# One-core encoder layer: projection weights planned in one list and loaded one projection ahead, and the last convolution chunk's taps in one piece

## The chip, the cores and the metric

The kernel runs on one core of one Trainium2 chip. The metric is the device time of one execution in microseconds (us). TensorE is called PE, VectorE DVE, ScalarE ACT, GpSimd POOL; SP issues the transfers (DMAs).

## What is computed

One encoder layer over 1552 tokens of 1024 channels: 16 meta tokens, a prompt of 512 and a sample of 1024, with shared weights. Cut to what matters:

```python
u = rms_norm(h, pre_g)
z = einsum('bld,de->ble', u, w_in)
c_val, c_glu, c_gate, q, k, v, a_gate = split(z)          # seven blocks of 1024 columns
conv_out = swish(layer_norm(dwconv31(c_val * sigmoid(c_glu)) + conv_b)) * silu(c_gate)
o_meta, o_grid = neighbourhood_attention(q, k, v, rel_bias)
att = concat(o_meta, o_grid) * silu(a_gate)
return h + rms_norm(concat(conv_out, att) @ w_out, post_g)
```

All is fp32. The products are made of split operands: an operand is rounded to a high part, and what is missing is its low part; each product is three matmuls (high·high, low·high, high·low).

## The kernel before

**Stages** (times of the span). Until 42 us the tokens are normalised and transposed; from 42 to 691 us the convolution branch runs; from 691 to 1222 us eight pairs of heads, each with its k and q projections, scores, softmax and weighted sum (`po`); from 1222 us the output product.

**A projection.** `w_in` is used in blocks of 128 output columns, each a weight of 512 KB. `load_w` (line 120) issues its transfer into `wraw` (SP), ACT casts it to the high part `whi` (line 115), POOL subtracts to get the low part `wlo` (line 116). `wraw`, `whi` and `wlo` have two buffers each, so a third weight waits until the first of the three has been used up. `proj` (line 128) then runs 24 matmuls into one PSUM tile `mm`, in the order high, low, high for each of 8 slices. Numbers below: val c is block c, glu c block 8+c, c_gate c block 16+c, q p block 24+p, k p block 32+p, a_gate p block 40+p ("ag p").

**The convolution stage.** Eight chunks of 128 channels. `conv_proj` (line 180) makes glu (4 tiles of 272, 256, 512 and 512 tokens, each through a sigmoid `sg` on ACT) and val (4 tiles, multiplied with `sg` into `ub` by DVE). `conv_taps` (line 218) is a 31-tap convolution: tap 0 by ACT (line 221), the other 30 by DVE, each reading the `z` the one before has written (line 223). `conv_stats` (line 237) subtracts a mean (`zc`, DVE), squares it (`zq`, ACT) and adds both into `acc` and `accsq`, on POOL or DVE. While DVE runs chunk c's taps, PE runs `stream(c)` (line 373): fillers (v units, c_gate, and ag 0 to 6) for about 44 us, then glu and val of chunk c+1. In chunk 7 the rest of the fillers run: two tiles of ag3, then ag4, ag5 and ag6.

**The last chunk** (line 388). For chunks 1 to 6 the taps are one piece, 128x1536. In chunk 7 `LASTP` makes two pieces: tokens 0 to 511 (128x512), whose statistics go to POOL, and 512 to 1535 (128x1024), whose statistics go to DVE.

**The end of the stage** (lines 419 to 426): six matmuls `ss` sum `acc` and `accsq` over channels; the rows leave through ACT and SP to `std`. The attention of a pair needs its k and q, the bias tables (`raw` from `ed`, added to `e` and `ei` by POOL, line 500) and v tiles (`vp`, `vt`, lines 528 and 531).

**What sets the order.** The Python code walks the work in the order above, with a generator for PE's side (`stream`) and one for DVE's (`convolve`), advanced by rough costs in us. A scheduler then places each engine's instructions by its own modelled times, so that the order on an engine can differ from that of the code; each engine runs its own list in order, and waits on semaphores.

Of the kernel before, what the change touches and what calls it, by code (L numbers as in the profile page):

```python
# [23 lines left out]
NPAIR = 8  # L24
# [4 lines left out]
MGROUPS = ((0, 272), (272, 528), (528, 1040), (1040, 1552))  # L29
# [11 lines left out]
NCG1 = 6  # L41
HOLD, EM1, NEW = 1, 13, 4
MLT = 1
NVS = 7
FILL = (0, 44, 44, 44, 44, 44, 44, 999)
NAG1 = 7
NXT = 4
LASTP = ((0, 1), (1, 3))
LAG = 1
IVM = 3  # L50
TAP_US = 1.85
CONV_ORDER = tuple((k, i) for k in "gv" for i in range(4))
BMM, BSS, BTP = 3, 2, 2
VPB = 1
# [13 lines left out]
def tile_encoder(ctx: ExitStack, tc: tile.TileContext, mt, xn, w_main, w_v, wo, cw, cb, lg, lb, pg, postg, rbt, rmask, y):  # L68
    nc = tc.nc
# [50 lines left out]
    def load_w(ec):  # L120
# [4 lines left out]
        split_w(raw, hi, lo)  # L125
        return hi, lo

    def proj(ps, hi, lo, c0, c1):
        n = c1 - c0
        uh, ul = u_cols(c0, c1)  # L130
        for dc in range(DC):
            for i, (w, u) in enumerate(((hi, uh), (lo, uh), (hi, ul))):
                nc.tensor.matmul(ps[:, :n], lhsT=w[:, dc, :], rhs=u[dc // 4][:, dc % 4, :],  # L133
                                 start=(dc == 0 and i == 0), stop=(dc == DC - 1 and i == 2))
# [40 lines left out]
    um = vpool.tile([128, DC, 32], F32, name="um")  # L175
    nc.gpsimd.memset(um, 0.0)
    ubs = [cpool.tile([128, 3, UBS], F32, name=f"ub{i}") for i in range(2)]
    w0 = {}

    def conv_proj(c, order):  # L180
        ub = ubs[c % 2]
        gh, gl = w0.pop(8 + c) if 8 + c in w0 else load_w(8 + c)
        val = [w0.pop(c) if c in w0 else None]
        sgs = {}

        def glu(i):
            c0, c1 = MGROUPS[i]
            psg = ps_mm.tile([128, 512], F32, name="mm", tag="mm")
            proj(psg, gh, gl, c0, c1)
            sgs[i] = cpool.tile([128, c1 - c0], F32, name=f"sg{i}")  # L190
            nc.scalar.activation(out=sgs[i], in_=psg[:, :c1 - c0], func=AF.Sigmoid)

        def value(i):
            if val[0] is None:
                val[0] = load_w(c)
            c0, c1 = MGROUPS[i]
            sg = sgs.pop(i)
            psv = ps_mm.tile([128, 512], F32, name="mm", tag="mm")
            proj(psv, *val[0], c0, c1)
            for name, a, b, off in pieces(c0, c1):  # L200
                if name == "m":
                    nc.vector.tensor_tensor(out=ub[:, 0, 0:15], in0=psv[:, 1:16], in1=sg[:, 1:16], op=ALU.mult)
                    nc.gpsimd.tensor_copy(out=ub[:, 1, 0:15], in_=ub[:, 0, 0:15])
                    continue
                seg = "pab".index(name)
                b0, nb = off // 64, (b - a) // 64
                o = ub[:, seg, 15:527].rearrange("p (r b c) -> p b r c", r=8, b=8)[:, b0:b0 + nb]
                nc.vector.tensor_tensor(out=o, in0=psv[:, a:b].rearrange("p (b r c) -> p b r c", r=8, c=8),
                                        in1=sg[:, a:b].rearrange("p (b r c) -> p b r c", r=8, c=8), op=ALU.mult)

        for kind, i in order:
            (glu if kind == "g" else value)(i)
            if kind == "v" and i == 3:
                nc.gpsimd.tensor_copy(out=ub[:, 1, 527:542], in_=ub[:, 2, 15:30])
                nc.gpsimd.tensor_copy(out=ub[:, 2, 0:15], in_=ub[:, 1, 512:527])
            yield 24 * (MGROUPS[i][1] - MGROUPS[i][0]) * 0.00045
# [10 lines left out]
    def new_z():  # L227
        return zpool.tile([128, 3, 512], F32, name="z", bufs=2)
# [64 lines left out]
                yield 2.8  # L293

    def c_gate(cs):
        ws = [load_w(16 + c) for c in cs]
        if cs[0] < 3:
            vws[cs[0] + 1] = load_v(cs[0] + 1)
            v_meta(cs[0] + 1, vws[cs[0] + 1][0])
        for g in range(3):  # L300
            for c, (wh, wl) in zip(cs, ws):
                ps = ps_mm.tile([128, 512], F32, name="mm", tag="mm")
                proj(ps, wh, wl, 16 + g * 512, 16 + g * 512 + 512)
                gt = gpool.tile([128, 512], F32, name="ag", tag="ag", bufs=2)
                nc.scalar.copy(out=gt, in_=ps)
                nc.sync.dma_start(cgd[g][c], gt)
                yield 5.5

    def a_gate(p):
        wah, wal = load_w(40 + p)  # L310
        for g in range(3):
            ps = ps_mm.tile([128, 512], F32, name="mm", tag="mm")
            proj(ps, wah, wal, 16 + g * 512, 16 + g * 512 + 512)
            gt = gpool.tile([128, 512], F32, name="ag", tag="ag", bufs=2)
            nc.scalar.copy(out=gt, in_=ps)
            nc.sync.dma_start(agd[g][p], gt)
            yield 5.5
# [12 lines left out]
    fill = fillers()  # L330
# [8 lines left out]
    with tc.tile_pool(name="start", bufs=2, side="right", reuse_waits="tile") as sp:  # L339
        gb = sp.tile([128, D], F32, name="gb", bufs=1)  # L340
        for i, s in enumerate((1, 0) + tuple(range(2, 13))):
            prenorm(s, sp, gb)
            if i == 0:
                vws[0] = load_v(0)
                vraw0 = vws[0][0]
            if i == IVM:
                v_meta(0, vraw0)
            if LAG <= i < LAG + NVS:
                next(fill)
            if s == 5:  # L350
                w0[8] = load_w(8)
                w0[0] = load_w(0)
        for dst, src in ((cw_sb, cw), (cb_sb, cb), (lg_sb, lg), (lb_sb, lb), (rm_sb, rmask)):
            nc.sync.dma_start(dst, src)
    zpool = es1.enter_context(tc.tile_pool(name="zpool", bufs=1, reuse_waits="tile"))
# [3 lines left out]
    z = new_z()  # L359
# [12 lines left out]

    def stream(c):

        t = 0.0
        while t < FILL[c]:
            dt = next(fill, None)
            if dt is None:
                break
            t += dt  # L380
            yield dt
        if c < 7:
            yield from conv_proj(c + 1, CONV_ORDER)

    def convolve(c, z):

        if c > 0:
            for a, b in ((0, 3),) if c < 7 else LASTP:
                for _ in conv_taps(c, z, a, b):
                    yield TAP_US * (b - a) / 3  # L390
                if c == 7:
                    for i in range(a, b):
                        conv_stats(c, z, i, nc.vector if b == 3 else nc.gpsimd)
        else:
            conv_mean(z)
        if c < 7:
            for i in range(3):
                conv_stats(c, z, i, nc.gpsimd)
                yield TAP_US / 3
        if 1 <= c <= 6:  # L400
            expand_bias(c - 1, last_load[0])

    for c in range(8):
        if c > 0:
            z = new_z()
# [56 lines left out]
    last = [None]  # L462

    def pair_proj(p):
        wkh, wkl = load_w(32 + p)
        pool = apool if p % 2 else kpool
        kh = pool.tile([128, 8, NROW, 8], F32R, name="kh")
        kl = pool.tile([128, 8, NROW, 8], F32R, name="kl")
        for (c0, c1) in MGROUPS:
            ps = ps_mm.tile([128, 512], F32, name="mm", tag="mm")  # L470
            proj(ps, wkh, wkl, c0, c1)
            for name, a, b, off in pieces(c0, c1):
                if name == "m":
                    src = ps[:, 0:16].rearrange("p (x c) -> p x c", x=2).unsqueeze(1).broadcast_to([128, 4, 2, 8])
                    for row in (ROW_M, ROW_M2):
                        oh = kh[:, :, row, :].rearrange("p (y x) c -> p y x c", x=2)
                        ol = kl[:, :, row, :].rearrange("p (y x) c -> p y x c", x=2)
                        nc.scalar.copy(out=oh, in_=src)
                        nc.vector.tensor_tensor(out=ol, in0=src, in1=oh.bitcast(F32), op=ALU.subtract)
                    continue  # L480
                row = {"p": ROW_P, "a": ROW_A, "b": ROW_B}[name]
                b0, nb = off // 64, (b - a) // 64
                src = ps[:, a:b].rearrange("p (b x) -> p b x", x=64)
                oh = kh[:, b0:b0 + nb, row:row + 8, :].rearrange("p b r c -> p b (r c)")
                ol = kl[:, b0:b0 + nb, row:row + 8, :].rearrange("p b r c -> p b (r c)")
# [91 lines left out]
    for p in range(NPAIR):  # L577
        e_build(p)
        kh, kl = pair_proj(p)
        wqh, wql = load_w(24 + p)  # L580
        for g in range(3):
            qs = pair_q(p, wqh, wql, g)
            attention(p, g, kh, kl, qs)
        if p >= NAG1:
            for _ in a_gate(p):
                pass
# [195 lines left out]
```

## Time and profile before

| | |
|---|---|
| three runs | 1515.48, 1517.15, 1517.20 us; median 1517.15 us |
| profiled execution | 1517.83 us, its span 1516.1 us (1.7 us lie around the span) |
| PE busy | 1460.5 us, 96% of the span |
| DVE, ACT, POOL busy | 1006.9 us (66%), 585.3 us (39%), 351.4 us (23%) |
| granted TensorE clock | 0.986 of full speed, mean |
| weights loaded, cast and split in this way | 48 |

The profiled execution is 0.7 us above the median. A line of a timeline gives the start, the duration, the engine, the line of the kernel and the tiles; a number in brackets is the time the engine stood idle just before, with what ended that. PE's matmuls overlap, so the step from one start to the next is the price of one, not its duration.

### The profile page before, as it was taken

How to read it: one execution, taken by the hardware profiler on the slowest of the kernel's cores; microseconds unless marked ns; L12 is line 12 of the kernel's file. 1: busy time of each engine (PE TensorE's matmuls, PEld its weight loads, DVE VectorE, ACT ScalarE, POOL GpSimd, SP SyncE). 2: the span in 40 equal slices, each digit the busy share in tenths (PEclk: the TensorE clock that was granted, in tenths of full speed). 3: DMA queues.
4: the chain of work that ended last, by engine and by line, in shares of the span. 5: the costliest groups of instructions: out<-in, count | busy, mean ns of one | idle time of the engine just before them, and what ended most of it. 6: DMA issues, size and time to landing. Idle time of an engine off the chain costs nothing.

```text
span 1516.1 us, 24156 instructions
## 1 busy us (share of the span) xinstructions
PE 1460.5 (96%) x9506; PEld 1241.3 (82%) x9506; DVE 1006.9 (66%) x1739; ACT 585.3 (39%) x1296; POOL 351.4 (23%) x258
## 2 busy tenths in 40 slices
PE   7998999999999898969999999999999979999998
PEld 6987898989988787757888888888887867888876
DVE  7699989797959698991545545546555557553442
ACT  7312121122111121112544545545544567456652
POOL 1133232233031323562121111111210002122121
PEclk9999999999999999989999999999999999999999
DMA  8013123141122131024112222212222367454542
GB/s 274 24 49 104 46 59 112 53 137 61 48 74 90 38 103 63 29 87 122 52 56 65 63 61 82 66 44 61 86 58 81 119 189 218 131 169 131 148 137 75
DMA packets 124470, 138.91 MB, mean 92 GB/s; under 512 B 8110, under 2 KB 96430, under 8 KB 124356
## 3 DMA queue, kind: packets, MB, share of 16 engines
q1 hardware_dynamic: 124356, 137.36, 29.6%
q8 instruction: 75, 1.23, 0.3%
q14 instruction: 39, 0.32, 0.1%
HBM read 99.05 MB, written 42.71 MB: 94 GB/s over the span
## 4 chain that ended last, share of the span: by engine, by line
PE 76%; DVE 9%; DMA 6%; issue 4%; POOL 2%; ACT 2%; SPq 0%; DVEq 0%; POOLq 0%; ACTq 0%
PE mm L133 49%; PE mm L286 8%; DVE z L223 5%; PE ss L548 5%; PE po L571 5%; PE tp L564 4%; PE py L682 4%; DMA mb<-std 2%; DMA mx<-zs 2%; POOL wlo L116 1%; POOL ml L655 1%; DMA yo<-in_wo 1%; DVE mx L653 1%; DVE mx L649 1%; DVE mx L648 1%
## 5 line engine op out<-in xcount | busy, mean ns | idle before, releaser
L133 PE MATMUL mm<-uw,whi 128*128 128x512 f32 (+2 forms) x2688 | 757.2, 364 | 3.2 <-ACT whi L115 3.2
L133 PEld LDWEIGHTS mm<-uw,whi 128*128 128x128 f32 x2688 | 485.1, 190 | 83.7 <-ACT whi L115 4.9
L223 DVE SCALAR_TENSOR_TENSOR z<-ub,cw_sb,z 128x1536 f32<-128x1536 f32 (+2 forms) x300 | 507.7, 1710 | 23.4 <-ACT z L221 15.2
L133 PE MATMUL mm<-uw,wlo 128*128 128x512 f32 (+2 forms) x1344 | 488.4, 364 | 18.1 <-POOL wlo L116 18.1
L133 PEld LDWEIGHTS mm<-uw,wlo 128*128 128x128 f32 x1344 | 255.6, 190 | 56.8 <-POOL wlo L116 19.1
L116 POOL TENSOR_TENSOR wlo<-wraw,whi 128x1024 fp32r<-128x1024 f32 x48 | 150.0, 3126 | 437.9 <-ACT whi L115 433.0
L682 PE MATMUL py<-uw,mh 128*128 128x512 f32 x576 | 180.0, 394 | 6.8 <-ACT mh L654 6.2
L286 PE MATMUL mm<-vh,uw 128*128 128x256 f32 x768 | 141.9, 284 | 1.1 <-ACT uw L158 0.6
L566 ACT COPY pT<-tp 108x256 f32<-108x256 f32 (+4 forms) x192 | 76.1, 425 | 153.4 <-PE tp L564 146.9
L682 PEld LDWEIGHTS py<-uw,mh 128*128 128x128 f32 x576 | 108.8, 189 | 31.1 <-ACT mh L654 6.4
L286 PEld LDWEIGHTS mm<-vh,uw 128*128 128x128 f32 x768 | 119.4, 190 | 3.3 <-ACT uw L158 1.0
L559 ACT ACTIVATE pt<-pt,sm 128x216 f32<-128x216 f32 (+4 forms) x192 | 96.9, 505 | 46.3 <-DVE sm L558 44.6
L682 PE MATMUL py<-uw,ml 128*128 128x512 f32 x288 | 113.2, 394 | 0.8 <-POOL ml L655 0.8
L556 DVE CUSTOM_DVE_ANT_0 pt<-ss,ei 128x216 f32<-128x216 f32 (+2 forms) x144 | 60.8, 439 | 77.7 <-PE ss L548 73.7
L655 POOL TENSOR_TENSOR ml<-mx,mh 128x1024 fp32r<-128x1024 f32 x22 | 54.4, 2490 | 245.5 <-ACT mh L654 245.5
L286 PE MATMUL mm<-vl,uw 128*128 128x256 f32 x384 | 108.1, 282 | 0.0
L561 DVE TENSOR_SCALAR pt<-pt,sm 128x216 f32<-128x216 f32 (+4 forms) x192 | 76.2, 397 | 5.5
L564 PE MATMUL tp<-ident,pt 128*96 128x128 f32 (+2 forms) x480 | 78.8, 282 | 0.0
L286 PEld LDWEIGHTS mm<-vl,uw 128*128 128x128 f32 x384 | 72.7, 189 | 0.8 <-issue 0.5
L115 ACT CAST whi<-wraw 128x1024 fp32r<-128x1024 f32 x48 | 50.3, 1048 | 48.9 <-PE mm L133 32.8
L571 PEld LDWEIGHTS po<-pT,vt 96*64 96x64 f32 (+1 forms) x1408 | 47.8, 137 | 23.5 <-issue 13.4
L682 PEld LDWEIGHTS py<-uw,ml 128*128 128x128 f32 x288 | 54.4, 189 | 13.6 <-POOL ml L655 1.3
(147 smaller groups left out, 1630.7 us busy)
## 6 DMA issues: line engine op xcount, KB each, us to landing
wraw<-in_w_main SPq DMA_DIRECT2D x48, 512.0 KB
xt<-in_xn SPq DMA_DIRECT2D x12, 512.0 KB
vd<-vs SPq DMA_DIRECT2D x96, 64.0 KB
zs<-zc SPq DMA_DIRECT2D x24, 256.0 KB
cgd<-ag SPq DMA_DIRECT2D x24, 256.0 KB
agd<-ag SPq DMA_DIRECT2D x24, 256.0 KB
mad<-mo SPq DMA_DIRECT2D x24, 256.0 KB
mx<-zs SPq DMA_DIRECT2D x12, 512.0 KB
```

Source lines behind the costliest of these rows:

```text
L116: eng.tensor_tensor(out=lo, in0=raw, in1=hi.bitcast(F32), op=ALU.subtract)
L133: nc.tensor.matmul(ps[:, :n], lhsT=w[:, dc, :], rhs=u[dc // 4][:, dc % 4, :], start=(dc == 0 and i == 0), stop=(dc == DC - 1 and i == 2))
L223: nc.vector.scalar_tensor_tensor(out=zv, in0=ub[:, a:b, k:k + 512], scalar=cw_sb[:, c, k:k + 1], in1=zv, op0=ALU.mult, op1=ALU.add)
L286: nc.tensor.matmul(ps[:, :256], lhsT=u[dc // 4][:, dc % 4, :], rhs=w[dc // 4][:, dc % 4, :], start=(dc == 0 and i == 0), stop=(dc == DC - ...
L548: nc.tensor.matmul(ss[:, :nk * w], lhsT=q[:, jj].rearrange("p h x -> p (h x)"), rhs=k[:, b0:b0 + nk, ra:ra + rn, :].rearrange("p b r c -> ...
L559: last[0] = nc.scalar.activation(out=pv, in_=pv, func=AF.Exp, bias=sm[:, 1:2], scale=1.0, accum_out=sm[:, 2:3])
L561: nc.vector.tensor_scalar(out=pv, in0=pv, scalar1=sm[:, 3:4], scalar2=None, op0=ALU.mult)
L564: nc.tensor.transpose(out=tp[:kt, k * 128:k * 128 + 128], in_=pv[:, k * kt:k * kt + kt], identity=ident)
L566: nc.scalar.copy(out=pT[:kt, :nt * 128], in_=tp[:kt, :nt * 128])
L571: nc.tensor.matmul(po[hs, j, :], lhsT=v, rhs=pT[:kt, k * 128 + h * 64:k * 128 + h * 64 + 64], start=(k == 0), stop=(k == nt - 1))
L655: (nc.vector if t < MLT else nc.gpsimd).tensor_tensor(out=ml, in0=mx, in1=mh.bitcast(F32), op=ALU.subtract)
L682: nc.tensor.matmul(pss[hf], lhsT=m[e // 8][:, e % 8], rhs=w[e][:, hf * 512:hf * 512 + 512], start=(e == 0 and i == 0), stop=(e == 15 and i ...
```

## The change

The fillers and projections of all chunks are now laid out in a list, `_plan`, which also returns the sequence `wseq` of the weights that they use, in order. `use_w` takes the place of `load_w` in every projection of the two stages: it hands out the weight that was loaded ahead, or loads it, and then loads the next one of the list. The generators `stream` and `convolve` follow the list. `LASTP` is gone: the last chunk's taps are one piece of 128x1536, and all its statistics go to POOL.

```diff
+def _plan():
...
+    base = {"g": 8, "x": 0, "cg": 16, "ag": 40}
+    seq = [8, 0]
+    for units in chunks:
+        for kind, x, _, _ in units:
+            if kind != "v" and seq[-1] != base[kind] + x:
+                seq.append(base[kind] + x)
+    for p in range(NPAIR):
+        seq += [32 + p, 24 + p] + [40 + p] * (p >= NAG1)
+    return first, chunks, seq + list(range(16 + NCG1, 24))
...
+    def use_w(ec):
+
+        w = ahead.pop(ec) if ec in ahead else load_w(ec)
+        i = wseq.index(ec) + 1
+        if i < len(wseq) and wseq[i] not in ahead:
+            ahead[wseq[i]] = load_w(wseq[i])
+        return w
...
         def value(i):
             if val[0] is None:
-                val[0] = load_w(c)
+                val[0] = use_w(c)
...
     def a_gate(p):
-        wah, wal = load_w(40 + p)
+        wah, wal = use_w(40 + p)
...
     def convolve(c, z):
 
         if c > 0:
-            for a, b in ((0, 3),) if c < 7 else LASTP:
-                for _ in conv_taps(c, z, a, b):
-                    yield TAP_US * (b - a) / 3
-                if c == 7:
-                    for i in range(a, b):
-                        conv_stats(c, z, i, nc.vector if b == 3 else nc.gpsimd)
+            for _ in conv_taps(c, z, 0, 3):
+                yield TAP_US
         else:
             conv_mean(z)
-        if c < 7:
-            for i in range(3):
-                conv_stats(c, z, i, nc.gpsimd)
-                yield TAP_US / 3
+        for i in range(3):
+            conv_stats(c, z, i, nc.gpsimd)
+            yield TAP_US / 3
...
-        wqh, wql = load_w(24 + p)
+        wqh, wql = use_w(24 + p)
```

Two entries of `wseq` stand in it twice: blocks 40 (ag0) and 43 (ag3), whose three tiles are divided between two chunks, with glu and val of the next chunk between them. `use_w` looks up the first place of a block. So `use_w` of val6 loads ag0 a second time, into buffers that no matmul reads, and `use_w` of val7 does so with ag3; ag1 and ag4 are then loaded when they are asked for, together with ag2 and ag5. That makes 50 loads, casts and splits in place of 48.

**ACT, end of glu6 to the second tile of ag1.** Before; `whi_4439` is val6, `whi_4586` ag1, `whi_4685` ag2, `sg3` glu6's last sigmoid:

```order
L191 ACTIVATE sg2_4380<-mm_4355 128x512
L191 ACTIVATE sg3_4410<-mm_4385 128x512
L115 CAST whi_4439<-wraw_4437 128x1024
L245 ACTIVATE zq_4415<-zc_4412 128x512
L245 ACTIVATE zq_4422<-zc_4419 128x512
L245 ACTIVATE zq_4429<-zc_4426 128x512
L115 CAST whi_4586<-wraw_4584 128x1024
L221 ACTIVATE z_4551<-ub0_129,cb_sb_96,cw_sb_95 128x1536
L315 COPY ag_4577<-mm_4552 128x512
L115 CAST whi_4685<-wraw_4683 128x1024
L315 COPY ag_4615<-mm_4590 128x512
```

Of the change; `whi_4300` is val6, `whi_4445` the second ag0, `whi_4592` ag1, `whi_4598` ag2:

```order
L233 ACTIVATE sg2_4386<-mm_4361 128x512
L146 CAST whi_4300<-wraw_4298 128x1024
L233 ACTIVATE sg3_4416<-mm_4391 128x512
L287 ACTIVATE zq_4421<-zc_4418 128x512
L287 ACTIVATE zq_4428<-zc_4425 128x512
L287 ACTIVATE zq_4435<-zc_4432 128x512
L146 CAST whi_4445<-wraw_4443 128x1024
L263 ACTIVATE z_4557<-ub0_129,cb_sb_96,cw_sb_95 128x1536
L146 CAST whi_4592<-wraw_4590 128x1024
L357 COPY ag_4583<-mm_4558 128x512
L146 CAST whi_4598<-wraw_4596 128x1024
L357 COPY ag_4627<-mm_4602 128x512
```

The cast of val6 now stands ahead of the last sigmoid; the cast of the second ag0 has the place that ag1's had, and ag1's stands behind tap 0. On POOL the subtractions stand in the same order. val7, the second ag3 and ag4 show the same pattern in chunk 7.

**DVE, the last chunk.** Before, from its second 512-token product on (`ub_130`); the pair of rows 128x512 and 128x1024 then goes on, one tap at a time:

```order
L208 TENSOR_TENSOR ub_130<-mm,sg_4937 128x8x8x8
L223 SCALAR_TENSOR_TENSOR z<-ub_130,cw_sb,z 128x512 x2
L223 SCALAR_TENSOR_TENSOR z<-ub_130,cw_sb,z 128x1024
L223 SCALAR_TENSOR_TENSOR z<-ub_130,cw_sb,z 128x512
L223 SCALAR_TENSOR_TENSOR z<-ub_130,cw_sb,z 128x1024
```

and at its end:

```order
L240 TENSOR_TENSOR zc<-z,m_982 128x512
L223 SCALAR_TENSOR_TENSOR z<-ub_130,cw_sb,z 128x1024 x12
L240 TENSOR_TENSOR zc<-z,m_982 128x512 x2
L246 TENSOR_TENSOR acc<-acc,zc 128x512 x2
L247 TENSOR_TENSOR accsq<-accsq,zq 128x512 x2
L479 TENSOR_TENSOR kl<-mm,kh 128x8x8 x2
```

Of the change, the whole chunk:

```order
L250 TENSOR_TENSOR ub_130<-mm,sg_4919 128x8x8x8
L250 TENSOR_TENSOR ub_130<-mm,sg_4949 128x8x8x8
L265 SCALAR_TENSOR_TENSOR z<-ub_130,cw_sb,z 128x1536 x30
L282 TENSOR_TENSOR zc<-z,m_988 128x512 x3
L511 TENSOR_TENSOR kl<-mm,kh 128x8x8 x2
```

The taps of 128x512, which began before the last product and alternated with those of 128x1024, have become 30 of 128x1536 behind all products, and the additions have left DVE.

**PE, the first sum of the statistics.** Before, behind the last matmul of ag6 (`whi_5377`), ahead of k0 (`whi_5588`):

```order
L133 MATMUL mm_5446<-uw_118,wlo_5378 128x512
L133 MATMUL mm_5446<-uw_120,whi_5377 128x512
L423 MATMUL ss_5488<-acc_983,ones_87 1x512
L423 MATMUL ss_5493<-accsq_984,ones_87 1x512
L133 MATMUL mm_5594<-uw_109,whi_5588 128x272
```

Of the change; `whi_5360` and `wlo_5361` are k0, and `mm_5639` is its third tile:

```order
L175 MATMUL mm_5639<-uw_114,wlo_5361 128x512
L175 MATMUL mm_5639<-uw_116,whi_5360 128x512
L455 MATMUL ss_5475<-acc_989,ones_87 1x512
L175 MATMUL mm_5639<-uw_114,whi_5360 128x512
L175 MATMUL mm_5639<-uw_114,wlo_5361 128x512
```

The first `ss` now stands 66 matmuls into k0 (24 of 272, 24 of 256 and 18 of 512 tokens); the others follow within k0's last two tiles and q0.

## Rows read from the trace of the kernel before

**Rows 1.** Stretches of the span; columns: window, length, busy time and instructions per engine, granted clock, DMA
```profile
155.00:507.00 352.00, 352.00 (x2169) 313.67 (x2168) 306.26 (x175) 66.08 (x113) 98.86 (x65) 0.99 0.24 73
507.00:596.00 89.00, 81.50 (x390) 68.44 (x388) 71.41 (x40) 16.53 (x23) 25.28 (x15) 0.96 0.21 71
643.00:657.00 14.00, 0.97 (x4) 0.54 (x3) 14.00 (x14) 0.00 (x0) 13.54 (x1) 0.65 0.00 0
760.00:1222.00 462.00, 461.40 (x4021) 388.77 (x4019) 251.05 (x1035) 231.84 (x679) 65.94 (x74) 1.00 0.25 75
```

**Rows 2.** PE's waits, 400 to 691 us: total us, times, longest us
```profile
PE mm L133 <- POOL wlo L116: 18.1, 3, 13.0
PE mm L133 <- ACT whi L115: 3.2, 2, 1.6
```

**Rows 3.** PE's timeline at ag5
```profile
656.60 0.80 PE L133 MATMUL mm<-uw,wlo 128*128 128x512 f32 x1 [13.03 <-POOL wlo L116]
...
660.60 0.49 PE L133 MATMUL mm<-uw,wlo 128*128 128x512 f32 x1
```

**Rows 4.** POOL's timeline: splits of ag1 and ag2, additions of chunk 6, split of ag5
```profile
532.33 2.41 POOL L116 TENSOR_TENSOR wlo<-wraw,whi 128x1024 fp32r<-128x1024 f32 x1 [0.17 <-POOL ub L214]
538.19 2.40 POOL L116 TENSOR_TENSOR wlo<-wraw,whi 128x1024 fp32r<-128x1024 f32 x1 [3.46 <-ACT whi L115]
...
599.14 3.34 POOL L246 TENSOR_TENSOR acc<-acc,zc 128x512 f32<-128x512 f32 x2 [2.42 <-DVE zc L240]
...
628.51 28.03 POOL L116 TENSOR_TENSOR wlo<-wraw,whi 128x1024 fp32r<-128x1024 f32 x1 [8.29 <-ACT whi L115]
```

**Rows 5.** DVE's timeline: taps of chunk 5's end, of chunk 6, of chunk 7 (rows join taps of both sizes)
```profile
498.94 11.09 DVE L223 SCALAR_TENSOR_TENSOR z<-ub,cw_sb,z 128x1536 f32<-128x1536 f32 x6
...
533.81 64.52 DVE L223 SCALAR_TENSOR_TENSOR z<-ub,cw_sb,z 128x1536 f32<-128x1536 f32 x30 [1.91 <-ACT z L221]
...
617.24 36.50 DVE L223 SCALAR_TENSOR_TENSOR z<-ub,cw_sb,z 128x512 f32<-128x512 f32 x37
...
654.25 21.73 DVE L223 SCALAR_TENSOR_TENSOR z<-ub,cw_sb,z 128x1024 f32<-128x1024 f32 x12
```

**Rows 6.** PE's timeline at val6
```profile
509.10 0.74 PE L133 MATMUL mm<-uw,whi 128*128 128x272 f32 x3 [1.62 <-ACT whi L115]
512.28 0.59 PE L133 MATMUL mm<-uw,wlo 128*128 128x272 f32 x1 [2.44 <-POOL wlo L116]
...
517.56 0.28 PE L133 MATMUL mm<-uw,wlo 128*128 128x256 f32 x1
...
517.91 0.28 PE L133 MATMUL mm<-uw,wlo 128*128 128x256 f32 x1
```

**Rows 7.** ACT's timeline: ends of glu6, val6, val7, ag6 and k0
```profile
507.51 0.60 ACT L191 ACTIVATE sg<-mm 128x512 f32<-128x512 f32 x1 [4.84 <-PE mm L133]
508.01 1.04 ACT L115 CAST whi<-wraw 128x1024 fp32r<-128x1024 f32 x1
...
531.14 1.05 ACT L115 CAST whi<-wraw 128x1024 fp32r<-128x1024 f32 x1 [10.55 <-PE mm L133]
532.09 1.68 ACT L221 ACTIVATE z<-ub,cb_sb,cw_sb 128x1536 f32<-128x1536 f32 x1
...
616.02 1.05 ACT L115 CAST whi<-wraw 128x1024 fp32r<-128x1024 f32 x1 [8.81 <-PE mm L133]
...
691.50 0.59 ACT L315 COPY ag<-mm 128x512 f32<-128x512 f32 x1 [2.89 <-PE mm L133]
...
714.87 0.59 ACT L486 CAST kh<-mm 128x512 fp32r<-128x512 f32 x1 [4.85 <-PE mm L133]
```

**Rows 8.** SP's queue: loads of v tiles, loads of the weights behind k1
```profile
706.82 1.78 SPq L528 DMA_DIRECT2D vp<-vd  x4
...
718.91 19.12 SPq L122 DMA_DIRECT2D wraw<-in_w_main  x2
```

**Rows 9.** PE's timeline: the first weighted sum of the attention
```profile
736.08 0.69 PE L571 MATMUL po<-pT,vp 108*64 108x64 f32 x16
```

More of the change, by code (lines that the diff above doesn't have):

```diff
@@ L47 @@
 NXT = 4
-LASTP = ((0, 1), (1, 3))
 LAG = 1
@@ L51 @@
 TAP_US = 1.85
+def _plan():
+    fill = []
+    for qv in range(4):
+        fill += [("v", qv, t, 2.8) for t in range(12)]
+        fill += [("cg", qv, g, 5.5) for g in range(3)]
+    fill += [("cg", c, g, 5.5) for c in range(4, NCG1) for g in range(3)]
+    fill += [("ag", p, g, 5.5) for p in range(NAG1) for g in range(3)]
+    first, fill = fill[:NVS], fill[NVS:]
+    chunks = []
+    for c in range(8):
+        t, units = 0.0, []
+        while fill and t < FILL[c]:
+            units.append(fill.pop(0))
+            t += units[-1][3]
+        if c < 7:
+            units += [(k, c + 1, i, 24 * (MGROUPS[i][1] - MGROUPS[i][0]) * 0.00045) for k in "gx" for i in range(4)]
+        chunks.append(units)
+    assert not fill
+    base = {"g": 8, "x": 0, "cg": 16, "ag": 40}
[7 more added lines that the diff above has]
+    return first, chunks, seq + list(range(16 + NCG1, 24))
 CONV_ORDER = tuple((k, i) for k in "gv" for i in range(4))
@@ L126, in load_w @@
         return hi, lo
+    first_units, chunk_units, wseq = _plan()
+    ahead = {}
+    def use_w(ec):
[4 more added lines that the diff above has]
+        return w
     def proj(ps, hi, lo, c0, c1):
@@ L177, in tile_encoder @@
     ubs = [cpool.tile([128, 3, UBS], F32, name=f"ub{i}") for i in range(2)]
-    w0 = {}
     def conv_proj(c, order):
         ub = ubs[c % 2]
-        gh, gl = w0.pop(8 + c) if 8 + c in w0 else load_w(8 + c)
-        val = [w0.pop(c) if c in w0 else None]
+        gate, val = [None], [None]
         sgs = {}
@@ L187, in glu @@
             c0, c1 = MGROUPS[i]
+            if gate[0] is None:
+                gate[0] = use_w(8 + c)
             psg = ps_mm.tile([128, 512], F32, name="mm", tag="mm")
-            proj(psg, gh, gl, c0, c1)
+            proj(psg, *gate[0], c0, c1)
             sgs[i] = cpool.tile([128, c1 - c0], F32, name=f"sg{i}")
@@ L295, in c_gate @@
     def c_gate(cs):
-        ws = [load_w(16 + c) for c in cs]
+        ws = [use_w(16 + c) for c in cs]
         if cs[0] < 3:
@@ L350, in tile_encoder @@
             if s == 5:
-                w0[8] = load_w(8)
-                w0[0] = load_w(0)
+                ahead[8] = load_w(8)
+                ahead[0] = load_w(0)
         for dst, src in ((cw_sb, cw), (cb_sb, cb), (lg_sb, lg), (lb_sb, lb), (rm_sb, rmask)):
@@ L373, in stream @@
     def stream(c):
[L375 to L380, printed above, removed]
+        conv = conv_proj(c + 1, CONV_ORDER) if c < 7 else None
+        for kind, _, _, dt in chunk_units[c]:
+            next(conv if kind in "gx" else fill)
             yield dt
-        if c < 7:
-            yield from conv_proj(c + 1, CONV_ORDER)
     def convolve(c, z):
         if c > 0:
-            for a, b in ((0, 3),) if c < 7 else LASTP:
-                for _ in conv_taps(c, z, a, b):
-                    yield TAP_US * (b - a) / 3
-                if c == 7:
-                    for i in range(a, b):
-                        conv_stats(c, z, i, nc.vector if b == 3 else nc.gpsimd)
+            for _ in conv_taps(c, z, 0, 3):
+                yield TAP_US
         else:
             conv_mean(z)
-        if c < 7:
-            for i in range(3):
-                conv_stats(c, z, i, nc.gpsimd)
-                yield TAP_US / 3
+        for i in range(3):
+            conv_stats(c, z, i, nc.gpsimd)
+            yield TAP_US / 3
         if 1 <= c <= 6:
@@ L464, in pair_proj @@
     def pair_proj(p):
-        wkh, wkl = load_w(32 + p)
+        wkh, wkl = use_w(32 + p)
         pool = apool if p % 2 else kpool
```

## The prediction, made before the changed kernel ran

> **What bounds the kernel now.** I read the stretches first. From 155 to 507 us PE is busy all 352.00 us, and in the attention 461.40 of 462 [rows 1]: neither stretch has time that earlier weights could give back. Between them it idles 7.5 us in 507 to 596 and 13.0 us in 643 to 657, where the granted clock falls to 0.96 and 0.65 [rows 1]. The waits name the causes: three waits on a low part of a weight, 18.1 us with one of 13.0, and two on a high part, 3.2 us [rows 2]. So the place is the end of the convolution stage, and PE sets the time: 21.3 us of waits on weights, plus what the clock loses after each.
>
> The longest wait is not a late load. The split of ag5 begins on POOL at 628.51 and takes 28.03 us, where those of ag1 and ag2 took 2.41 and 2.40 [rows 4]. Meanwhile DVE runs 37 taps without a pause, 617.24 to 653.74; these are the taps of two independent pieces in turn. Then 128x1024 taps follow alone, each needing the one before, from 654.25 [rows 5], and the split ends at 656.54. The split of ag2 (538.19) fell among 128x1536 taps, which depend on each other too, and got in at once. I read this as: POOL gets its operands when DVE pauses between dependent taps, not while DVE always has a ready one.
>
> The Trainium skill has a rule against this reading (SBUF — State Buffer, section "SBUF: two separate sides"): DVE and GpSimd share one pair of ports by an exclusive lock, held for a whole instruction, and the loser blocks until it ends. By it the split would wait for one tap, at most 1.8 us (21.73/12, rows 5), the rest would have another cause, and a change of taps would save nothing there. The row of 28.03 us does not bear that out; a cause apart from the taps is rival B.
>
> **The change, part by part.**
>
> *One piece of taps in chunk 7.* All 30 taps depend on each other, as in chunk 6. The split of ag5 should then take 2 to 4 us like the other 47, within the 10.9 us of two tiles of ag4. What goes is PE's wait, 13.03 us [rows 3], and its half-clock stretch: the three triples from 656.60 to 660.60 took 4.00 us [rows 3], where a full-speed triple of 256 columns takes 0.35 (517.56 to 517.91, rows 6 show it), so 0.70 for 512 and 2.1 for three; loss 1.9, with the triple's rest 2.0. Together **−15.0 us**. Bounds: 0, if the split stays long, and −15.3.
>
> *val6 and val7.* They are asked for a projection early, which doesn't help: of the two buffers ag0 (of which a tile is still to come) holds one, and glu6 the other until its last matmul; at val7 these are ag3 and glu7. So the chain stays: glu6's end, cast, split, PE. Only the cast moves ahead of the last sigmoid, which now delays it from 507.51 to 508.01 [rows 7]: 0.5 us each, **−1.0 us**. What stays per place is 1.1 + 2.44 us of wait, and the slow stretch behind it: 23 matmuls of 272 columns from 512.28 to 517.56 took 5.28 us [rows 6], at full speed 23 × 0.35/3 × 272/256 = 2.85; loss 2.4. Since the two waits stay nearly as long, I let the clock fall again. Bounds: 0 and, if it stays up at both, −4.8 more.
>
> *ag1 on demand.* Let E be the end of val6, 531.1 [rows 7]. Now the cast of ag1 starts there and its split is done at 534.74 [rows 4], before ag0's last tile ends at E+5.45. In the change the useless cast comes first (1.05), then tap 0 (1.68), then ag1's cast, which also waits for the useless split: it begins near E+3.7, ends E+4.75, and the split of 2.41 ends E+7.2 to 7.9, the later where it first waits for a tap of 1.85. PE has ag0's tile to E+5.45 and three high matmuls to E+6.2. **+1.5 us**; bounds 1.0 and 2.9, and 2.4 more if the clock falls. ag4 has the same order, but two tiles of ag3, 10.9 us, cover it: 0.
>
> *The tail of the stage.* Let E7 be val7's end, 616.0 [rows 7]. DVE loses the start before E7, but 30 taps at 11.09/6 = 1.85 [rows 5] are 55.5 us. In chunk 6 they took 64.52 [rows 5], 9.0 more, with five splits beside them: 1.8 a split. Six splits now: 55.5 + 10.8 = 66.3, from E7+2.7 (as 533.81 stands to 531.1) to E7+69.0; then `zc`, 0.7, and the first addition on POOL, half of 3.34 [rows 4]: E7+71.4. PE now ends ag6 75.4 us after E7 (691.4, rows 7), without the 15.0 us 60.4, and reaches the first `ss` 66 matmuls later (24 × 0.124 + 24 × 0.117 + 18 × 0.233 = 10.0): E7+70.4. A wait of 1.0, and about as much again behind it, because the next `kh` casts stand behind `zq` on ACT and k0's last tile needs their buffer: **+2.0 us**; bounds 0 and 5.
>
> *Into the attention.* k0 ends at 714.9 [rows 7]. The cast of k1 comes there, its split is done some 4 us later, and on SP the load of k2 waits for that, ahead of `std`, `raw` and the v tiles. Now the v tiles are issued at 706.82 [rows 8] and used at 736.08 [rows 9]. Issued at about 720 instead, they keep 16 of these 29 us, and I take 0; bounds 0 and 3, the lower because nothing waits on them now.
>
> *The rest.* The 36 splits and casts elsewhere are hidden now and stay so; the two useless loads, 1.05 us of ACT and 2.4 of POOL each, are in the terms above. Additions moved from DVE to POOL are in the tail.
>
> Sum: −15.0 − 1.0 + 1.5 + 2.0 = −12.5. Against the profiled execution: 1517.8 − 12.5 = 1505.3. This lies 0.7 above the median, so on the median's scale **1504.6 us**.
>
> **The rivals.**
>
> *A. All three waits go.* If the weights really are ahead, 21.3 us of waits [rows 2] and 2.4 + 2.4 + 2.0 of slow clock go, less 2.0 in the tail: 1517.8 − 28.1 + 2.0 = 1491.7, or 1491.0 on the median's scale. Against: two buffers and the order, in which the first three high matmuls of val6 still stand together.
>
> *B. The long split has another cause* than the independent taps, and stays: −1.0 + 1.5 + 2.0 = +2.5, 1519.6, no difference that can be told. For it: the trace shows one such split only. Against it: the 28.03 us and where they ended. The rule of the Trainium skill above would give this case.
>
> *C. DVE becomes the bound.* One-piece taps finish later than I have it, because each split takes more of a tap. To cancel 12.5 us the last tap must end near E7+81.5: 2.6 us a tap, where chunk 6 had 64.52/30 = 2.15 [rows 5]. Then about 1517.
>
> *D. Slower: SP's queue.* Each weight is asked for a projection earlier, and a load on SP waits there for its buffer with the loads of `raw` and the v tiles behind it; `po` would wait in each pair. It decides from (12.5 + 3.0)/8 = 1.9 us a pair; at 3 us, 1504.6 + 24 = 1528.6. For it: two weight loads already hold the queue for 19.12 us [rows 8]. Against: PE idles 0.6 us in the whole stage all the same [rows 1], and the loads there keep two buffers as before.
>
> **How the numbers follow.** A measurement of this kernel can tell about 0.2%, 3.0 us, from no change. My forecast in its own range has 0.79, A 0.05, B 0.05, C 0.04, D 0.07. The range 1498 to 1512 is the forecast's own: down 4.8 if the clock does not fall at val6 and val7, and 1.8 of the two new waits; up 3.8 for ag1 with a slow stretch, 3.0 for the tail, rounded. Faster: 0.79 + 0.05 = 0.84; no difference: 0.05 + 0.04 = 0.09; slower: 0.07.
>
> **What would show it.** Right: the split of ag5 takes 2 to 4 us; PE has no wait at ag5; two waits each at val6 and val7, about 1.1 and 2.4; one of 1 to 3 us at ag1; one at the first `ss`; 50 splits. Wrong, if ag5's split stays above 10 us, if val6 and val7 have no waits (A), or if `po` waits in many pairs (D).

## The result and the profile after

The changed kernel takes 1504.53 us (median of four runs, 1504.43 to 1507.96) against 1517.02 us: a ratio of 0.9925, 95% interval 0.9908 to 0.9943, 12.5 us faster. The forecast was 1504.6 us in a range of 1498 to 1512. The profiled execution took 1504.52 us, 13.3 us less than that of before, with a span of 1502.7 us and a mean granted clock of 0.992.

The stretches of the span of the changed kernel, the windows of rows 1:

```profile
155.00:507.00 352.00, 349.22 (x2159) 311.22 (x2158) 305.56 (x174) 65.27 (x112) 99.17 (x66) 1.00 0.24 73
507.00:596.00 89.00, 82.05 (x387) 68.38 (x387) 71.43 (x40) 17.30 (x24) 29.24 (x16) 0.96 0.23 77
643.00:657.00 14.00, 14.00 (x63) 11.48 (x62) 13.69 (x8) 2.71 (x4) 2.92 (x1) 1.00 0.26 94
760.00:1222.00 462.00, 459.42 (x3992) 385.27 (x3990) 251.97 (x1020) 236.19 (x681) 62.58 (x70) 1.00 0.25 74
```

PE is busy all 14 us from 643 to 657, at full clock, where it had 0.97 us at 0.65 [rows 1]; 507 to 596 has hardly changed. PE's waits from 400 to 700 us, beside [rows 2]:

```profile
PE mm L175 <- POOL wlo L147: 6.5, 3, 3.0
PE mm L175 <- ACT whi L146: 2.4, 2, 1.2
PE ss L455 <- POOL acc L288: 1.5, 1, 1.5
PE mm L175 <- ACT ag L357: 0.2, 1, 0.2
```

The wait of 13.0 us is gone; those at val6 and val7 are left, and two are new, at ag1 and at the first `ss`. POOL's timeline, the splits of val6, ag1 and ag5:

```profile
507.71 3.56 POOL L147 TENSOR_TENSOR wlo<-wraw,whi 128x1024 fp32r<-128x1024 f32 x1 [24.37 <-ACT whi L146]
...
534.90 2.67 POOL L147 TENSOR_TENSOR wlo<-wraw,whi 128x1024 fp32r<-128x1024 f32 x1 [1.16 <-ACT whi L146]
...
628.24 2.56 POOL L147 TENSOR_TENSOR wlo<-wraw,whi 128x1024 fp32r<-128x1024 f32 x1 [5.03 <-ACT whi L146]
```

ag5's split takes 2.56 us in place of 28.03 [rows 4]. PE's timeline at val6, at ag1 and at the first `ss`:

```profile
507.68 1.00 PE L175 MATMUL mm<-uw,whi 128*128 128x272 f32 x3 [1.18 <-ACT whi L146]
511.31 0.59 PE L175 MATMUL mm<-uw,wlo 128*128 128x272 f32 x1 [2.63 <-POOL wlo L147]
...
516.56 0.28 PE L175 MATMUL mm<-uw,wlo 128*128 128x256 f32 x1
...
536.23 0.50 PE L175 MATMUL mm<-uw,whi 128*128 128x512 f32 x1 [0.21 <-ACT ag L357]
537.63 0.51 PE L175 MATMUL mm<-uw,wlo 128*128 128x512 f32 x1 [0.90 <-POOL wlo L147]
...
687.39 1.02 PE L455 MATMUL ss<-acc,ones 128*1 128x512 f32 x2 [1.47 <-POOL acc L288]
```

At val6 the chain is that of [rows 6]: two waits, then 23 matmuls from 511.31 to 516.56 at the same slow pace. ACT's timeline, the ends of glu6, val6, val7 and ag6 (the release by PE in brackets), beside [rows 7]:

```profile
506.58 1.04 ACT L146 CAST whi<-wraw 128x1024 fp32r<-128x1024 f32 x1 [4.88 <-PE mm L175]
...
530.15 1.05 ACT L146 CAST whi<-wraw 128x1024 fp32r<-128x1024 f32 x1 [10.52 <-PE mm L175]
...
615.74 1.06 ACT L146 CAST whi<-wraw 128x1024 fp32r<-128x1024 f32 x1 [7.98 <-PE mm L175]
...
676.07 0.59 ACT L357 COPY ag<-mm 128x512 f32<-128x512 f32 x1 [4.85 <-PE mm L175]
```

Against before, the end of glu6 comes 0.93 us earlier, that of val6 0.99, that of val7 0.28, that of ag6 15.43. So 15.15 us were won between val7 and ag6, 0.7 lost between val6 and val7, and the 0.93 ahead of glu6 are a sum. Won: PE's wait for chunk 0's taps, near 150 us, fell from 6.6 to 2.3 us, and the granted clock from 110 to 200 us is 1.00 in place of 0.96. Lost: a wait near 122 us grew from 0.4 to 2.4 us, and 155 to 507 us, without a gap before, has 2.8 us of them now. How the 0.93 divides among these was not worked out. DVE's timeline, the taps of chunks 6 and 7, and PE's first weighted sum of the attention:

```profile
532.82 66.39 DVE L265 SCALAR_TENSOR_TENSOR z<-ub,cw_sb,z 128x1536 f32<-128x1536 f32 x30 [1.91 <-ACT z L263]
...
618.40 66.49 DVE L265 SCALAR_TENSOR_TENSOR z<-ub,cw_sb,z 128x1536 f32<-128x1536 f32 x30 [1.89 <-ACT z L263]
```

```profile
723.35 0.45 PE L603 MATMUL po<-pT,vp 108*64 108x64 f32 x8
```

Both chunks took two us more than the 64.52 of chunk 6 before [rows 5]. The first `po` comes 12.7 us earlier than before [rows 9]; 2.7 of the 15.4 us were given back in the tail, and 0.7 come again later.

### The profile page after: what moved, and what is told of

Same layout as the page of the kernel before. It is cut to its first block, busy times and chain, and to the rows that moved or that the text cites. A ratio compares the mean times of both kernels' runs of the same rounds, so it can differ in the third digit from the quotient of the medians.

```text
span 1502.7 us, 24143 instructions
## 1 busy us (share of the span) xinstructions
PE 1459.5 (97%) x9506; PEld 1238.6 (82%) x9506; DVE 1004.6 (67%) x1705; ACT 587.1 (39%) x1297; POOL 339.8 (23%) x264
## 4 chain that ended last, share of the span: by engine, by line
PE 76%; DVE 19%; ACT 2%; DMA 1%; POOL 1%; issue 1%; SPq 0%; DVEq 0%; ACTq 0%; POOLq 0%
PE mm L175 39%; DVE z L265 17%; PE py L714 16%; PE mm L328 5%; PE ss L580 5%; PE po L603 5%; PE tp L596 4%; POOL wlo L147 1%; DMA yo<-in_wo 1%; ACT whi L146 0%; DVE zc L282 0%; PE ss L455 0%; PE ss L197 0%; DMA gb<-in_pg 0%; PE tp L197 0%
## 5 line engine op out<-in xcount | busy, mean ns | idle before, releaser
L147 POOL TENSOR_TENSOR wlo<-wraw,whi 128x1024 fp32r<-128x1024 f32 x50 | 136.2, 2725 | 410.9 <-ACT whi L146 410.1
L580 PE MATMUL ss<-kh,qh 128*128 128x264 f32 (+3 forms) x192 | 65.2, 339 | 0.0
```

Of the source, the lines that this page charges most:

```text
L147: eng.tensor_tensor(out=lo, in0=raw, in1=hi.bitcast(F32), op=ALU.subtract)
L580: nc.tensor.matmul(ss[:, :nk * w], lhsT=q[:, jj].rearrange("p h x -> p (h x)"), rhs=k[:, b0:b0 + nk, ra:ra + rn, :].rearrange("p b r c -> ...
```

## The experiments

The theory was that of the prediction: while DVE runs taps of two independent pieces in turn, POOL gets no operands, and the wait at ag5 is the price. A request is the start of POOL's row for a split: it gets in when the row is about as long as usual (2.4 to 4 us), and stays out when the row lasts on. The first rival: the plan, by loading earlier, removed the wait. All ratios are to the kernel before, run on the same chip.

**1. The last chunk alone** (`one_piece_only`): the kernel before with

```diff
-            for a, b in ((0, 3),) if c < 7 else LASTP:
...
+            for _ in conv_taps(c, z, 0, 3):
+                yield TAP_US
```

and all statistics on POOL. Expected:

> The kernel before with nothing changed but the last chunk: its taps are one piece of 128x1536 and all its statistics go to POOL; weights are loaded as before, 48 of them. Theory (independent taps on DVE keep POOL from its operands): the split of ag5 takes 2 to 4 us in place of 28.03, PE does not wait at ag5, the waits at val6 and val7 stay (about 4.1 us each), there is none at ag1, one of 1 to 2 us at the first ss: 1504, between 1502 and 1506. Rival (the earlier loads of the plan removed the wait): the wait at ag5 stays, 1516 to 1520.

Measured: 1502.07 us, ratio 0.9910 (0.9895 to 0.9925). PE's waits from 400 to 720 us and POOL's split of ag5:

```profile
PE mm L133 <- POOL wlo L116: 5.1, 2, 2.6
PE mm L133 <- ACT whi L115: 3.2, 2, 1.6
```

```profile
626.99 2.40 POOL L116 TENSOR_TENSOR wlo<-wraw,whi 128x1024 fp32r<-128x1024 f32 x1 [8.89 <-ACT whi L115]
```

Without the plan the wait at ag5 is gone, and all of the gain is there: the plan adds none on top of the one piece (0.9910 without it, 0.9925 with it, intervals that overlap). The wait expected at the first `ss` is missing; that part of the expectation was wrong.

**2. The plan alone** (`plan_only`): the changed kernel with `LASTP` and its loop put back. Expected:

> The changed kernel with the last chunk's two pieces put back; the plan and use_w stay. Theory: the split of ag4 is now asked for where the taps of the two pieces begin to alternate (some 4.5 us behind val7's end), and gets no operands until the 128x512 piece ends some 38 us behind val7: it takes 30 us or more, PE waits at ag4 for about 28 us where it had two tiles of ag3 to do, and the kernel is slower than both, 1525 to 1537. Rival (the plan alone removed the wait): 1502 to 1507.

Measured: 1506.81 us, 0.9942 (0.9927 to 0.9957). The theory's forecast missed; the time lies in the rival's range. POOL's splits of ag4, ag5 and ag6, and DVE's alternating taps, which are those of before:

```profile
621.89 2.56 POOL L148 TENSOR_TENSOR wlo<-wraw,whi 128x1024 fp32r<-128x1024 f32 x1 [1.64 <-ACT whi L147]
627.30 3.01 POOL L148 TENSOR_TENSOR wlo<-wraw,whi 128x1024 fp32r<-128x1024 f32 x1 [2.85 <-ACT whi L147]
643.80 17.09 POOL L148 TENSOR_TENSOR wlo<-wraw,whi 128x1024 fp32r<-128x1024 f32 x1 [13.49 <-ACT whi L147]
```

```profile
619.46 38.63 DVE L266 SCALAR_TENSOR_TENSOR z<-ub,cw_sb,z 128x512 f32<-128x512 f32 x37
```

Two splits got in among the independent taps, the third stayed out for 17.09 us, and PE waited 2.1 us for that one. The plan did not ask for ag5 earlier: val7 ends here at 614.8 and the request comes 12.5 us later, exactly as in the kernel before (616.0 and 628.51). So the theory as a rule without exceptions falls. Of the rival only the number stands, not its reason, an earlier load: the kernel gained 9.3 us here because a request that came at the same place was let in.

**3. The same taps, the split elsewhere** (`ag5_split_on_dve`): the kernel before with

```diff
-        wah, wal = load_w(40 + p)
+        wah, wal = load_w(40 + p, nc.vector if p == 5 else None)
```

where the second argument is the engine of the subtraction. Expected:

> The kernel before with the subtraction that splits ag5 on DVE in place of POOL; taps in two pieces and loads as before. Theory: the wait at ag5 goes although the taps still alternate, and the next split on POOL, that of ag6, begins near 645 us while they alternate and takes some 10 us, which nothing waits for: 1501 to 1505. Rival (POOL is slow at that place for a reason of its own, or the weight comes late): the wait stays, 1515 to 1519; or ag6's split takes 2 to 4 us.

Measured: 1502.87 us, 0.9915 (0.9900 to 0.9930). DVE's split of ag5 and POOL's of ag6:

```profile
630.67 1.22 DVE L116 TENSOR_TENSOR wlo<-wraw,whi 128x1024 fp32r<-128x1024 f32 x1
```

```profile
644.07 12.98 POOL L116 TENSOR_TENSOR wlo<-wraw,whi 128x1024 fp32r<-128x1024 f32 x1 [24.54 <-ACT whi L115]
```

The weight was not late: split on DVE, it costs PE nothing. The next split on POOL stays out until the 128x512 taps end, as expected, and nothing waits for it.

**4. Two pieces in another chunk** (`chunk5_two_pieces`): the changed kernel with

```diff
-            for _ in conv_taps(c, z, 0, 3):
-                yield TAP_US
+            for a, b in ((0, 1), (1, 3)) if c == 5 else ((0, 3),):
+                for _ in conv_taps(c, z, a, b):
+                    yield TAP_US * (b - a) / 3
```

> The changed kernel with the taps of chunk 5 in two pieces, 128x512 and 128x1024; the last chunk stays in one. Theory: the long split is not a matter of the last chunk: the split of ag0, asked for when c_gate 4 ends, falls among alternating taps and takes about 20 us, PE waits for it some 6 us and the clock falls behind that: 1508 to 1515. Rival (the last chunk is special, or a split waits for one tap at most): no split over 5 us, 1503 to 1506.

Measured: 1513.40 us, 0.9980 (0.9970 to 0.9990), most of the gain given back. PE's waits from 400 to 720 us, and POOL's split of ag0:

```profile
PE mm L175 <- POOL wlo L147: 12.8, 4, 7.5
```

```profile
464.19 22.41 POOL L147 TENSOR_TENSOR wlo<-wraw,whi 128x1024 fp32r<-128x1024 f32 x1 [13.92 <-ACT whi L146]
```

The stall moves with the two pieces: a split that takes 22.41 us and a wait of 7.5 us stand where the changed kernel has neither (its split of ag0 took 2.40 us). This and experiment 1 show that the two pieces, 128x512 and 128x1024, bring the stall. They don't show that their independence alone does.

**5. What lets a request in.** The traces suggested the moment within a tap: requests 0.01 to 0.45 us behind the start of a 128x1024 tap had stayed out, those at 0.52 and 0.98 us had got in. Four kernels are the kernel before with ag5's cast begun again (`n` 2; 4; 8; 8 and 4), so that the request comes later:

```diff
+        for n in (4,) if ec == 45 else ():
+            nc.scalar.copy(out=hi[:, 0:n, :], in_=raw[:, 0:n, :])
         split_w(raw, hi, lo)
```

> The kernel before; ACT casts the first 256 columns of ag5's weight once more just ahead of the whole cast, so that POOL's request for the split comes some 0.3 us later; nothing else moves. In the traces so far a request that came up to 0.45 us behind the start of a 128x1024 tap stayed out while the independent taps ran (0.21 in the kernel before), and one that came 0.52 us or more behind it got in at the next tap. First theory (any request is kept out while independent taps alternate): split of 27 us or more, time 1514 to 1519. Second theory (the moment within the tap decides): the request comes 0.5 us into the tap, on the edge, either way.

> The same with 512 columns cast twice: POOL's request comes some 0.5 us later, 0.7 to 0.8 us into the 128x1024 tap. First theory (any request is kept out): split of 27 us, time 1514 to 1519. Second theory (the moment decides): it gets in at the next tap, the split takes 2.5 to 3.5 us, PE does not wait at ag5, time 1500 to 1505, though ACT does more than before.

> The same with the whole cast done twice: POOL's request comes some 0.95 us later, about 1.15 us into the 128x1024 tap, close to the start of the next 128x512 tap. First theory: split of 27 us, 1514 to 1519. Second theory: it gets in, 2.4 to 3.5 us, 1500 to 1505; if it is counted to the next tap, which has just begun, it stays out.

> The same with one and a half casts ahead: POOL's request comes some 1.5 us later, about 0.5 us into the 128x512 tap that follows, which holds for 0.66 us. First theory: split of 26 us, 1514 to 1519. Second theory, if the moment within any tap decides and not the 128x1024 tap alone: it gets in, 1500 to 1505.

Measured: 1516.20, 1516.62, 1515.46 and 1516.50 us, ratios 0.9997, 1.0003, 0.9995 and 1.0001, none clear of 1. POOL's split with 512 columns cast again:

```profile
627.84 27.37 POOL L116 TENSOR_TENSOR wlo<-wraw,whi 128x1024 fp32r<-128x1024 f32 x1 [8.96 <-ACT whi L115]
```

It comes 0.88 us behind the start of a 128x1024 tap and stays out. The other three took 27.59, 26.94 and 26.30 us; they came 0.66 us into a 128x1024 tap, 0.11 us into a 128x512 tap and 0.09 us into a 128x1024 tap. The last was meant to come 0.5 us into a 128x512 tap, so it doesn't test what it was built for. A request 0.66 us into a 128x1024 tap stayed out here, and one at 0.66 us gets in in experiment 6: the moment within a 128x1024 tap does not decide.

**6. The same shift where the request got in** (`plan_only_cast_later`): the kernel of experiment 2 with the loop of experiment 5, `n` 8 and 8. Expected:

> The kernel with the plan alone (two pieces in the last chunk), where ag4's and ag5's splits got in among the alternating taps; ACT casts ag5's weight two more times ahead of the cast that counts, so POOL's request comes some 2 us later, about 8.5 us behind the first alternating tap in place of 6.4. Theory now (a request gets in only soon after the taps have begun to alternate or DVE has stood still): the split of ag5 takes 25 us or more, PE waits for it some 13 us, 1518 to 1526. Rival (in that kernel the requests get in for another reason, whenever they come): split of 2.5 to 3.5 us, 1505 to 1509.

Measured: 1508.00 us, 0.9945 (0.9926 to 0.9964). POOL's split of ag5:

```profile
629.50 2.87 POOL L148 TENSOR_TENSOR wlo<-wraw,whi 128x1024 fp32r<-128x1024 f32 x1 [4.85 <-ACT whi L147]
```

It still gets in, 8.4 us behind the first alternating tap, where the request of the kernel before stayed out 7.6 us behind it. So the time since the taps began to alternate does not decide either.

**7. POOL busy shortly before** (`pool_kept_awake`): the kernel before with

```diff
+        if ec == 45:
+            nc.gpsimd.memset(lo[:, 0, 0:16].bitcast(F32), 0.0)
         split_w(raw, hi, lo)
```

> The kernel before, with one small POOL memset (128x16) into ag5's low part, which can run when ag3's last matmul is done, some 1.5 us ahead of the request for ag5's split; the loads, the taps and all other engines as before. What the traces show so far: among alternating independent taps the requests that stayed out came when POOL had been idle for 8.3 us or more, those that got in after 1.6, 2.9, 4.9 and (one exception) 9.4 us. Theory (a POOL that worked shortly before gets its turn): the split takes 2.5 to 3.5 us, no wait at ag5, 1500 to 1504. Rival (POOL's idle time is a coincidence): split of 27 us, 1514 to 1519; then what lets a request in stays open.

Measured: 1517.35 us, 1.0005 (0.9996 to 1.0015). POOL's timeline:

```profile
627.72 0.12 POOL L126 MEMSET wlo<- 128x16 f32 x1 [6.48 <-PE mm L135]
629.58 27.97 POOL L116 TENSOR_TENSOR wlo<-wraw,whi 128x1024 fp32r<-128x1024 f32 x1 [1.75 <-issue]
```

The memset ran at once, 1.75 us ahead of the request, and the split stayed out: POOL's idle time does not decide. What does stays open.

**Two other pieces in turn.** The trace of the kernel before has a second stretch of independent taps, which the prediction did not read: from 122 to 155 us DVE takes chunk 0's last 128x1024 taps and chunk 1's first 128x1536 taps in turn, without a pause. POOL's timeline and DVE's taps there (busy us and mean ns, then the idle time before them):

```profile
128.22 7.12 POOL L116 TENSOR_TENSOR vl<-wraw,vh 128x1024 fp32r<-128x1024 f32 x2 [7.31 <-ACT vh L115]
136.72 2.50 POOL L116 TENSOR_TENSOR wlo<-wraw,whi 128x1024 fp32r<-128x1024 f32 x1 [1.38 <-ACT whi L115]
148.62 2.66 POOL L116 TENSOR_TENSOR wlo<-wraw,whi 128x1024 fp32r<-128x1024 f32 x1 [9.40 <-ACT whi L115]
```

```profile
L223 DVE SCALAR_TENSOR_TENSOR z<-ub,cw_sb,z 128x1536 f32<-128x1536 f32 x8 | 18.7, 2334 | 0.0
L223 DVE SCALAR_TENSOR_TENSOR z<-ub,cw_sb,z 128x1024 f32<-128x1024 f32 x9 | 15.8, 1753 | 0.0
```

All four splits got in, in 2.50 to 3.80 us, and the taps went on in turn behind each. (The last of them is the exception of 9.4 us in the expectation of experiment 7.) The same stretch stands in all 14 traces, with 50 requests: 44 got in within one tap; the other six came 1.4 to 3 us before the stretch ended and began at its end. So taps that are independent and always ready don't keep POOL out by themselves. Nor do 128x512 taps that each need the one before: a split among those, at 617.21 us in the kernel before, took 2.41 us. POOL stayed out only where taps of 128x512 and 128x1024 took turns, and there in ten of 14 requests. Whether the sizes make the difference was not tried.

**8. Each weight once** (`each_weight_once`): the changed kernel with

```diff
-                seq.append(base[kind] + x)
+                if base[kind] + x not in seq:
+                    seq.append(base[kind] + x)
```

> The changed kernel with ag0 and ag3 listed once in the sequence: 48 loads, and ag1 and ag4 are the ones loaded ahead in val6 and val7; one-piece taps as in the change. Theory (the second loads of ag0 and ag3 cost PE some 1.5 us at ag1, two splits beside DVE's taps and what these delay in the tail): 2 to 3 us below the changed kernel, 1501 to 1503, and the waits at val6 and val7 stay as they are in the change. Rival (the second loads are what keeps val6 and val7 from being ahead): both waits go as well, 1488 to 1494. Second rival (the plan loses its 2 us elsewhere): 1504 to 1506.

Measured: 1501.17 us, 0.9903 (0.9888 to 0.9917). PE's waits from 400 to 700 us and DVE's taps of chunk 7:

```profile
PE mm L176 <- POOL wlo L148: 5.4, 2, 2.8
PE mm L176 <- ACT whi L147: 2.4, 2, 1.2
```

```profile
618.00 64.48 DVE L266 SCALAR_TENSOR_TENSOR z<-ub,cw_sb,z 128x1536 f32<-128x1536 f32 x30 [1.90 <-ACT z L264]
```

The waits at ag1 and at the first `ss` are gone, the taps take 2.0 us less, and the waits at val6 and val7 stay: the second loads are not what keeps val6 and val7 late. What they cost in all is not settled: 1.2 us by the spans of the two traces, 3.4 us by the medians, and the two intervals overlap.

**9. Buffers of their own for val6 and val7** (`val_own_buffers`): the kernel of experiment 8 with

```diff
+        if ec in (6, 7):
+            hi = vpool.tile([128, DC, 128], F32R, name="vh", bufs=2)
+            lo = vpool.tile([128, DC, 128], F32R, name="vl", bufs=2)
+        else:
```

> The same, each weight listed once, and the high and low parts of val6 and val7 lie in the buffers of the v weights, which are free by then, so that neither waits for a buffer that glu6 or glu7 holds. Theory (two buffers are what keeps the plan from loading val6 and val7 ahead): the waits there go (1.2 + 2.6 and 1.2 + 3.0 us, with some 2.5 us of half clock behind each), about 12 us below the kernel with each weight once, 1488 to 1492. Rival (DVE or ACT then holds the stage up): 1494 to 1500.

Measured: 1488.98 us, 0.9821 (0.9807 to 0.9835), the fastest of all. PE from 500 to 680 us, in two stretches:

```profile
500.00:590.00 90.00, 90.00 (x460) 76.74 (x459) 80.72 (x44) 17.24 (x24) 26.70 (x15) 1.00 0.21 70
590.00:680.00 90.00, 90.00 (x413) 72.32 (x411) 75.15 (x48) 18.23 (x29) 32.66 (x27) 1.00 0.23 79
```

PE never stops there and its clock does not fall: 12.2 us below experiment 8 on the same chip. This is what the plan gives once a buffer is free to load into. Whether such buffers would give it without the plan was not run.

## Why the prediction was right, and where not

| term | forecast, us | measured, us |
|---|---|---|
| ag5: wait and slow clock | −15.0 | −15.15 (val7's end to ag6's end) |
| val6 and val7: cast ahead of the last sigmoid | −1.0 | −0.06 and about −0.8, neither from the cast |
| ag1 on demand | +1.5 | +1.5 |
| tail and start of the attention | +2.0 | +2.7 at the first `po`, +2.0 at the end |
| ahead of glu6 | 0 | −0.93 |

**ag5.** The size is right to 0.15 us. Experiments 1, 3 and 4 show the mechanism in its parts: one piece alone removes the wait, the weight itself is in time, and two pieces in another chunk bring the stall there. What was too strong is the reading that POOL gets in only when DVE pauses: four splits in experiments 2 and 6 got in among independent taps of the same sizes, and all four from 122 to 155 us of the kernel before did, in rows that the prediction left unread. For the forecast nothing hung on that, as the taps of the changed chunk all depend on each other.

**val6 and val7.** As forecast, the cast came half a microsecond earlier (waits of 1.18 for 1.62) and the rest of the chain stayed. But this won nothing, so the term of −1.0 failed. At val6 the split took 3.56 us where it had taken 3.1, and the three high matmuls 1.00 where they had 0.74 [rows 6]: from glu6's end to the first low matmul it is 4.81 us for 4.80. PE's timeline at val7, before and then of the change:

```profile
593.43 0.39 PE L133 MATMUL mm<-uw,whi 128*128 128x272 f32 x1 [1.62 <-ACT whi L115]
...
596.77 0.60 PE L133 MATMUL mm<-uw,wlo 128*128 128x272 f32 x1 [2.59 <-POOL wlo L116]
```

```profile
593.66 0.39 PE L175 MATMUL mm<-uw,whi 128*128 128x272 f32 x1 [1.18 <-ACT whi L146]
...
597.64 0.40 PE L175 MATMUL mm<-uw,wlo 128*128 128x272 f32 x1 [2.98 <-POOL wlo L147]
```

From glu7's end (where the first wait begins) to the first low matmul it is 5.16 us for 4.96. What val7 won came behind that, from the clock: the granted clock from 593 to 604 us is 0.84, where it was 0.69. Before, then of the change:

```profile
593.00:604.00 11.00, 7.97 (x40) 7.66 (x41) 8.78 (x7) 1.25 (x3) 8.12 (x5) 0.69 0.35 117
```

```profile
593.00:604.00 11.00, 7.36 (x42) 6.84 (x43) 9.62 (x8) 1.74 (x3) 7.89 (x4) 0.84 0.25 77
```

The forecast let the clock fall as before at both places; that it fell for less time at val7 is luck, and no run here shows why. Experiment 9 shows that the wait hangs on the buffers: with buffers of their own it is gone. PE's order changed with them, the first low matmul standing behind one high one there and not behind three, so the order's own share is not shown.

**ag1.** Cast 3.63 us behind val6's end (forecast 3.7), split done at 7.4 (7.2 to 7.9), waits of 0.21 and 0.90. PE's steps there, from one start to the next, are 0.60 and 1.41 us where one usually is 0.23; that makes some 1.5 us more. The granted clock stayed at 1.00 (529 to 545 us), so the slow stretch that the forecast allowed for did not come. Experiment 8 has no such wait.

**The tail.** Last tap 69.2 us behind val7's end (forecast 69.0), first addition done at 71.6 (71.4), a wait of 1.47 at `ss` (1.0). Experiments 1 and 8, with two splits fewer, have no such wait: it is the price of the second loads, not of the one piece.

**The rivals.** A (all weights ahead) did not come, because of the two buffers; experiment 9 shows its size, 1489 us against the 1491 forecast for it. B fell with the changed kernel's own split of 2.56 us, and experiment 1 shows that the one piece is enough for it. C and D are not seen: the last tap is in time, and PE is busy 459.4 of 462 us in the attention. The total of 1504.6 is closer than its terms: the 0.93 us ahead of glu6 were not in it, and made up for what val6 did not give. That is luck, as is val7's share.

The Trainium skill (SBUF — State Buffer, section "SBUF: two separate sides") says that DVE and GpSimd hold their shared ports for one instruction each, and the other blocks until it ends. The splits that got in agree: the tap behind one in experiment 2 took 2.9 us for 0.75. Ten splits that waited 13 to 28 us, over many taps, do not, and the measurement decides. The prediction took 1.8 us for the one tap that a split would wait for by that rule; this averages in taps that a split had held up. A 128x1024 tap by itself takes 1.28 us, so the bound was too wide, and the argument stands.

## What to carry to other kernels

A wait on a helper engine's result is not yet a late load: compare the duration of the helper's instruction there with its usual one, and look at what the engine beside it was doing. Here a chain of dependent DVE instructions let POOL in within a step or two; two such chains in turn, of 128x512 and 128x1024, mostly did not for as long as both lasted, though two of 128x1024 and 128x1536 did. So look in the trace at how long the helper takes beside such a pair, and put it where no split is awaited. Loading a weight ahead gains only what a free buffer allows: write down who holds each buffer at the moment of the load, and see that no entry of the list stands twice.

## What was not expected of the hardware

Among independent taps of 128x512 and 128x1024, ten requests of POOL stayed out until the taps of one piece had ended (12.98 to 28.03 us, at three places of the program), and four got in within one tap (2.55 to 3.01 us). Among independent taps of 128x1024 and 128x1536, none of 50 stayed out beyond 5.2 us. Neither the moment within a 128x1024 tap, nor the time since the taps began to alternate, nor POOL's idle time before tells them apart (experiments 5, 6 and 7). Two differences were seen and not tried. Between the two kinds of stretch it is the size of the taps. Among the 14 requests: in experiment 2, where two got in, DVE's first 128x1024 tap began 0.03 us behind the end of ACT's tap 0; in the kernel before tap 0 ended 2.2 us earlier. This can't be the whole reason, as the third request of experiment 2 stayed out in the same run of taps.
